# A decoder layer in fp32: opening reordered, fold spread over blocks, and the last two token blocks convolved as one block of 1024 tokens

## The chip, the cores and the metric

The kernel runs on one core of one Trainium2 chip. A core has five engines that run at the same time, each through its own fixed order of instructions: TensorE (PE) for matmuls, VectorE (DVE) and ScalarE (ACT) for elementwise work, GpSimd (POOL), and SyncE (SP), which here issues most transfers between the memory outside the core (DRAM) and the core's own SBUF. Matmul results land in PSUM, which has eight banks of 128 x 512 fp32. The metric is the device time of one execution in microseconds (us). A profile shows one execution of its own.

## The reference

`x` is 4096 tokens by 1024 columns, in fp32; `c` is one conditioning vector. What is computed:

```
mod = silu(c) @ w_ada + b_ada;  shift, scale, gate = split(mod, 3)
h    = layer_norm(x) * (1 + scale) + shift
proj = h @ w_in + b_in                    # u_a 512 | z_a 512 | glu 1024 | z_b 512
y_a  = (group_linear(causal_pool(u_a) - u_a) + b_pool) * ls_pool * silu(z_a)
v    = glu[:512] * sigmoid(glu[512:])
v    = silu(layer_norm(causal_depthwise_conv31(v)) * ln_conv_g + ln_conv_b)
y_b  = (v @ w_pw + b_pw) * silu(z_b)
y    = concat(y_a, y_b) @ w_out + b_out
out  = layer_norm(2**0.25 * x + gate * y) * ln_post_g + ln_post_b
```

The pool takes trailing windows of 2, 4, 8 and 16 tokens, one for each of four column groups; the convolution has 31 taps per column.

## The kernel before

**Numbers.** Matmuls keep fp32 accuracy by splitting each operand into a high half (a rounded cast, `hi`) and a low half (the rest, `lo`): each product is three matmuls, hi x hi, hi x lo and lo x hi (`mm3`). ACT casts the high half, DVE subtracts to get the low half (`split`, lines 194 to 196). Nearly all matmuls are 128 x 128 by 128 x 512.

**Stages.** The tokens are cut into 8 blocks of 512 (`sb`), each with its even and odd tokens apart. Columns lie on the 128 partitions.

1. *Opening.* The modulation `mod_block` multiplies the eight row tiles of `w_ada` by `silu(c)` on DVE (`macc`, line 181) and sums over the partitions with matmuls against ones (line 186). Block 0's x is transposed on PE and modulated (`mod_turned`, lines 321 to 324); its low half needs `hs` from ACT. Rows of `w_in` are loaded and split (`wg0` to `wg7`). PE runs the first matmuls of block 0 row by row as these arrive.
2. *First phase*, blocks 0 to 7: `row_stats` of the next block (mean and variance of each token by ACT, `col_stats`, then one transfer `rD` and a broadcast `xbc`), `norm_T` (a load `xk` of the transposed x, normalized by DVE at lines 292 and 294), `mod_xT` (high half on ACT, line 303, low half on DVE, line 304, giving the tile `x`), then 8 chunks of 24 matmuls for the glu (`p`), and 2 chunks for half of z_b (`p1z`). At the end of block 0, `fold_u` multiplies the pool weights into the first 512 columns of `w_in`: for each of four groups a load `wT`, eight small matmuls in fp32 `fv` (two passes each) and a bias `bu`. At block 1, `mod_gate` computes the gate on DVE.
3. *Second phase*, blocks 0 to 7: ten chunks of 24 matmuls (`p2z`, `p2u`, `p2b`); the pools run on DVE.
4. *Convolution* (`conv`), on DVE throughout the first two phases for the blocks in `BLOCKS`: three accumulation chains (even tokens, odd tokens, and sums of both; tiles `cx`, `ca`), some 46 multiply-adds (line 576) over 256 columns for one block or 512 for two. `conv_ln` transposes the result (`cl`), takes statistics on ACT, and applies the layer norm at lines 606 and 607. Blocks 6 and 7 are *late units*: eight pieces (block, column group) of 512 tokens, with tiles `lv` (input), `lx`, `la` (result). `EARLY = 2` of them stand ahead of the output stage, the others, by `PERSB`, one behind each of its blocks 0 to 5, and each block's layer norm behind its fourth unit.
5. *Output stage*, blocks 0 to 7: `pw_stage` (48 matmuls `pw`, z on DVE at line 696, halves `yb`), `prep` of the next block (loads `t`, halves `vp` and `ya`), and four `out_tile`s of 48 matmuls each into two PSUM banks (`po`). Four banks let two tiles be open. DVE adds the residual (lines 705 and 731) and applies the last layer norm (lines 744 and 745).

**What sets the order.** The program is written as one sequence; a scheduler orders each engine's instructions once, when the kernel is built, by its own estimate of times and the dependences. On the chip every engine runs its list in that order: an instruction that waits holds all that stand behind it. Tiles of one tag share slots, and the load of a new tile waits until the last reader of the slot's old tile is done. The late units' lines are these:

```
    late = {6: [], 7: []}
    units = [(sb, m) for sb in (6, 7) for m in range(MC)]
    for _ in range(EARLY):
        sb, m = units.pop(0)
        late_unit(sb, m, late[sb])
```

## Time and profile before

| | |
|---|---|
| Three runs | 1394.03, 1406.32, 1406.85 us (median 1406.32) |
| The profiled execution | 1397.84 us |
| Its span (first to last instruction) | 1395.8 us |
| Mean granted clock of PE, as a share of full | 0.992 |
| PE busy | 1356.4 us, 97% |
| DVE busy | 1193.9 us, 86% |
| ACT, POOL busy | 432.6 us, 131.0 us |
| DMA | 243.81 MB, mean 175 GB/s |

The page cuts the span into 40 slices of 35 us; each digit is the busy share in tenths, 9 meaning 90% or more:

```profile
PE   4898999999999999999999999999999999999997
...
DVE  8688989983569999899899699999997899998754
```

PE is busy nearly everywhere but in the first slices. Engine busy times are sums of instruction times; neighbouring instructions on PE and DVE overlap a little, so what one costs its engine is read from start to start. A wait is named by what was waited for: "PE p L337 <- ACT x L321" is a matmul of line 337 into tile p that waited for ACT's tile x of line 321.

### The profile page before, as it was taken

The page shows a single profiled execution, that of the slowest core. Times are in us where ns is not written, and L with a number is a line of the kernel's source. Part 1 is how long each engine was busy: PE and PEld are TensorE (multiplying, and loading weights), DVE is VectorE, ACT ScalarE, POOL GpSimd, SP SyncE. Part 2 cuts the span into 40 slices and gives each one's busy share as a digit, 9 for nine tenths or more (in the row PEclk, how much of TensorE's full clock was granted, in tenths as well). Part 3 has the DMA queues.
Part 4 walks back from the last instruction along what each step waited for, and adds up shares of the span by engine and source line. Part 5 has one row for each costly group of instructions (what it writes and reads, how often), then busy time and mean ns, then how long its engine had stood idle before and what let it go on. Part 6 is the DMA issues. An engine that isn't in the chain of part 4 may idle for free.

```text
span 1395.8 us, 17137 instructions
## 1 busy us (share of the span) xinstructions
PE 1356.4 (97%) x6045; PEld 1118.5 (80%) x6045; DVE 1193.9 (86%) x2348; ACT 432.6 (31%) x772; POOL 131.0 (9%) x193
## 2 busy tenths in 40 slices
PE   4898999999999999999999999999999999999997
PEld 3777888888888888888888888888888888888886
DVE  8688989983569999899899699999997899998754
ACT  3544235245531231411114111343234131322310
POOL 1000000010100001210111110100111101001111
PEclk9999999999999999999999999999999999999999
DMA  9958677477563662360541723466444443433511
GB/s 323 328 180 323 214 275 267 163 267 235 180 249 124 226 194 83 131 233 23 182 139 59 234 67 123 131 203 196 157 167 148 139 159 118 162 129 130 186 61 76
DMA packets 113352, 243.81 MB, mean 175 GB/s; under 512 B 15027, under 2 KB 45555, under 8 KB 113267
## 3 DMA queue, kind: packets, MB, share of 16 engines
q1 hardware_dynamic: 103984, 209.15, 43.4%
q0 software_dynamic: 9216, 33.56, 7.2%
q8 instruction: 47, 0.77, 0.2%
q14 instruction: 39, 0.31, 0.1%
q10 hardware_dynamic: 66, 0.02, 0.0%
HBM read 156.65 MB, written 86.04 MB: 174 GB/s over the span
## 4 chain that ended last, share of the span: by engine, by line
PE 90%; DMA 5%; DVE 2%; ACT 2%; SPq 1%; issue 1%; DVEq 0%; ACTq 0%
PE po L713 25%; PE p L338 6%; PE p L339 6%; PE p L337 6%; PE p2z L338 4%; PE p2u L338 4%; PE p2z L337 4%; PE p2z L339 4%; PE p2u L337 4%; PE p2u L339 4%; PE pw L689 2%; PE pw L691 2%; PE pw L690 2%; PE p2b L338 2%; PE p2b L337 2%; PE p2b L339 2%
## 5 line engine op out<-in xcount | busy, mean ns | idle before, releaser
L576 DVE SCALAR_TENSOR_TENSOR cx<-cv,wdw,cx 128x513 f32<-128x513 f32 (+1 forms) x240 | 145.7, 613 | 0.7
L576 DVE SCALAR_TENSOR_TENSOR ca<-cx,wsum,ca 128x256 f32<-128x256 f32 (+1 forms) x240 | 143.7, 611 | 0.1
L576 DVE SCALAR_TENSOR_TENSOR ca<-cv,wdw,ca 128x256 f32<-128x256 f32 (+1 forms) x224 | 134.3, 611 | 0.0
L742 POOL TENSOR_TENSOR ors<-ove,mhalf 128x1 f32<-128x1 f32 x32 | 46.9, 1467 | 408.8 <-DVE ove L738 400.4
L736 ACT ACTIVATE ojk<-r,osm 128x1024 bf16<-128x1024 f32 x31 | 35.6, 1148 | 148.3 <-DVE osm L733 148.3
L332 POOL DMA_DIRECT2D x2r<-xD x64 | 34.8, 544 | 402.8 <-PE p2b L339 276.7
L731 DVE SCALAR_TENSOR_TENSOR r<-po,r 128x512 f32<-128x512 f32 x62 | 40.9, 687 | 22.0 <-PE po L713 21.9
L576 DVE SCALAR_TENSOR_TENSOR lx<-lv,wdw,lx 128x257 f32<-128x257 f32 x120 | 57.5, 479 | 0.0
L576 DVE SCALAR_TENSOR_TENSOR la<-lx,wsum,la 128x256 f32<-128x256 f32 x120 | 57.3, 478 | 0.0
L576 DVE SCALAR_TENSOR_TENSOR la<-lv,wdw,la 128x256 f32<-128x256 f32 x112 | 53.3, 478 | 0.0
L269 POOL TENSOR_TENSOR xcs<-smx,mhalf 128x1 f32<-128x1 f32 x28 | 20.7, 740 | 343.9 <-DVE smx L268 343.6
L517 ACT ACTIVATE sz<-p2z,cols 128x512 f32<-128x512 f32 x32 | 22.0, 688 | 95.6 <-PE p2z L339 95.5
L292 DVE TENSOR_TENSOR xk<-xk,xbc 128x1024 f32<-128x1024 f32 x28 | 34.1, 1222 | 17.2 <-DMA xk<-in_x_t_dram 17.2
L303 ACT ACTIVATE x<-xk,shc 128x512 fp32r<-128x512 f32 x56 | 38.0, 719 | 31.5 <-DVE xk L294 31.5
L304 DVE SCALAR_TENSOR_TENSOR x<-xk,shc,x 128x512 fp32r<-128x512 f32 x56 | 40.4, 749 | 8.3 <-ACT x L303 8.3
L524 ACT ACTIVATE u<-p2u,bu 128x512 f32<-128x512 f32 x32 | 22.0, 689 | 70.4 <-PE p2u L339 70.4
L745 DVE SCALAR_TENSOR_TENSOR r<-r,ors,b_bc 128x1024 f32<-128x1024 f32 (+1 forms) x33 | 41.1, 1248 | 3.2 <-POOL ors L742 3.1
L443 ACT ACTIVATE sg<-p,cols 128x512 f32<-128x512 f32 x32 | 21.9, 686 | 70.3 <-PE p L339 69.8
L265 ACT ACTIVATE x<-x 128x1024 f32<-128x1024 f32 x28 | 29.6, 1059 | 40.6 <-DMA x<-in_x_dram 39.7
L713 PE MATMUL po<-wo0h,ya 128*128 128x512 f32 x128 | 41.2, 392 | 0.0
L713 PE MATMUL po<-wo1h,ya 128*128 128x512 f32 x128 | 41.1, 390 | 0.0
L705 DVE SCALAR_TENSOR_TENSOR r<-r,gbo 128x1024 f32<-128x1024 f32 x32 | 39.0, 1218 | 1.7 <-DMA r<-in_x_dram 1.7
(360 smaller groups left out, 4107.4 us busy)
## 6 DMA issues: line engine op xcount, KB each, us to landing
x2r<-xD POOLq DMA_DIRECT2D x64, 512.0 KB, 7.3
xD<-x SPq DMA_DIRECT2D x56, 512.0 KB, 5.4
x<-in_x_dram SPq DMA_DIRECT2D x32, 512.0 KB, 6.8
r<-in_x_dram SPq DMA_DIRECT2D x32, 512.0 KB, 3.6
out_dram<-r SPq DMA_DIRECT2D x31, 512.0 KB, 2.6
xk<-in_x_t_dram SPq DMA_DIRECT2D x28, 512.0 KB, 8.2
wa<-in_w_ada_dram SPq DMA_DIRECT2D x32, 256.0 KB, 6.4
vD<-v SPq DMA_DIRECT2D x32, 256.0 KB, 2.2
```

The lines of the kernel that those rows point to most:

```text
L303: nc.scalar.activation(h2[:, 0, :], z, AF.Identity, bias=shc[:, k : k + 1])
L304: nc.vector.scalar_tensor_tensor(h2[:, 1, :], z, shc[:, k : k + 1], h2[:, 0, :].bitcast(F32), op0=ALU.add, op1=ALU.subtract)
L337: nc.tensor.matmul(ps, w[0], X[0], start=first, stop=False)
L338: nc.tensor.matmul(ps, w[0], X[1], start=False, stop=False)
L339: nc.tensor.matmul(ps, w[1], X[0], start=False, stop=last)
L576: nc.vector.scalar_tensor_tensor(dst, src, wt, dst, op0=ALU.mult, op1=ALU.add)
L705: xg = nc.vector.scalar_tensor_tensor(r, r, ALPHA, gbo, op0=ALU.mult, op1=ALU.add)
L713: mm = nc.tensor.matmul(po[h], lhs, Wo[k][wi][:, h * 512 : (h + 1) * 512], start=(k == 0 and wi == 0 and lhs is yh), stop=last)
L731: nc.vector.scalar_tensor_tensor(r[:, sl], po[h], 1.0, r[:, sl], op0=ALU.mult, op1=ALU.add, accum_out=sm[:, h : h + 1])
L736: nc.scalar.activation(jk, r, AF.Square, bias=sm[:, 2:3], accum_out=ss)
L742: nc.gpsimd.tensor_tensor(rs, ve, mhalf[:, 0:1], op=ALU.pow)
L745: nc.vector.scalar_tensor_tensor(r[:, sl], r[:, sl], rs, b_bc[:, sl], op0=ALU.mult, op1=ALU.add)
```

## The change

The changed kernel differs in eight places. Line numbers of the changed file are some 3 to 20 higher.

1. **Modulation.** `mod_block` accumulates six of eight row tiles on DVE; the last two are added on PE as further matmuls into the same sum, so that there are three for each one before.
2. **Rows of w_in.** Each of the 8 loads takes three quarters of the columns and is cast and subtracted by one operation on each engine (before: two). The last quarter comes by 8 later transfers of 128 KB (`w3r`) and 16 splits.
3. **x of block 1** is loaded in the opening, into four slots of the tag `ca` (`x_early`).
4. **Statistics.** `col_stats` leaves out two DVE and one POOL operation per tile: the factors go into ACT's scale, and into `s1n` and `lcg`; one power per block on POOL (`inv_root`).
5. **Stores** of block 0's x to `xD` stand behind the `xk` loads of block 1, where they stood behind the last modulation.
6. **Fold.** The four `fold_u` stand one each in blocks 2 to 5 of the first phase, their loads `wT` one block earlier; they use another PSUM tag and another SBUF tag for `wf`.
7. **Gate.** `mod_gate` moves from block 1 of the first phase to block 2 of the second.
8. **Late convolution.** Four units, one for each column group, of 1024 tokens (blocks 6 and 7 together). Unit 0 stands right before the output loop, units 1 to 3 behind its blocks 0 to 2, then one layer norm for both blocks. `lv` and `lx` take two of the six `ca` slots, of which `vp` takes four. `EARLY` and `PERSB` are gone.

The core of the diff:

```diff
@@ mod_block
-        for kt in range(KT):
+        nv = KT - 2
+        for kt in range(nv):
...
-                nc.tensor.matmul(ps[:, nk * i + j : nk * i + j + 1], acc[:, 1 - i, j * P : (j + 1) * P],
-                                 ones[:, 0:1], start=True, stop=True)
+                o = ps[:, nk * i + j : nk * i + j + 1]
+                sl = slice(j * P, (j + 1) * P)
+                nc.tensor.matmul(o, acc[:, 1 - i, sl], ones[:, 0:1], start=True, stop=False)
+                for kt in range(nv, KT):
+                    nc.tensor.matmul(o, wts[kt][:, 1 - i, sl], sc[:, kt : kt + 1], start=False, stop=kt == KT - 1)
@@ col_stats
-        nc.scalar.activation(src, src, AF.Identity, accum_out=sm[:, 0:1])
-        nc.vector.tensor_scalar(nmean, sm[:, 0:1], -1.0 / n, None, op0=ALU.mult)
-        nc.scalar.activation(src, src, AF.Square, bias=nmean, accum_out=sm[:, 1:2])
-        nc.vector.tensor_scalar(sm[:, 2:3], sm[:, 1:2], 1.0 / n, EPS, op0=ALU.mult, op1=ALU.add)
-        nc.gpsimd.tensor_tensor(rstd, sm[:, 2:3], mhalf[:, 0:1], op=ALU.pow)
+        nc.scalar.activation(src, src, AF.Identity, scale=-1.0 / n, accum_out=nmean)
+        nc.scalar.activation(src, src, AF.Square, bias=nmean, scale=-float(n), accum_out=ss)
+
+    def inv_root(ss, n):
+        nc.gpsimd.tensor_scalar(ss, ss, n * EPS, None, op0=ALU.add)
+        nc.gpsimd.tensor_tensor(ss, ss, mhalf[:, : ss.shape[1]], op=ALU.pow)
@@ opening
+    x_early = []
+    for t in range(TT):
+        xt = s2.tile([P, D], F32, tag="ca", bufs=6, name=f"x{TT + t}", padded_shape=[P, 2 * (HQ + T + 1)])
+        nc.sync.dma_start(xt, tok(xv, TT + t))
+        x_early.append(xt)
...
+        hi, lo = (both(t)[:, :, : 3 * P] for t in Wg[k])
+        nc.scalar.copy(hi, rows[k])
         xT.append(mod_turned(pb, k))
-        split_cols(k, 0, 3)
-        split_cols(k, 3, 4)
+        nc.vector.tensor_tensor(lo, rows[k], hi.bitcast(F32), op=ALU.subtract)
...
+    for q in range(2):
+        raw = wraw(f"w3r{q}").rearrange("p (k h c) -> p k h c", k=4, h=2)
+        for k in range(4):
+            nc.sync.dma_start(raw[:, k], both(w_in[(4 * q + k) * P : (4 * q + k + 1) * P, 8 * P : 16 * P])[:, :, 3 * P :])
+        for k in range(4):
+            hi, lo = (both(t)[:, :, 3 * P :] for t in Wg[4 * q + k])
+            split(hi, lo, raw[:, k])
@@ first phase, end of a block
-            for g in range(MC):
-                fold_u(g, wpl)
-        if sb == 1:
-            mod_gate(gbo)
...
+        if 1 <= sb <= MC:
+            wT = wraw(f"wT{sb - 1}")
+            nc.sync.dma_start(wT, w_in_t[(sb - 1) * P : sb * P, :])
+        if 2 <= sb <= MC + 1:
+            fold_u(sb - 2, wpl, wTs.pop(0))
+        if 1 <= sb <= MC:
+            wTs.append(wT)
@@ late units
+    def late_unit(m):
+        a = (lt.tile([P, 2 * T], F32, tag="la", bufs=2, name=f"la{m}") if m < 2 else
+             s2.tile([P, 2 * T], F32, tag="cv", bufs=2, name=f"la{m}", padded_shape=[P, 2 * (HQ + T + 1)]))
+        v = s2.tile([P, 2, HQ + T + 1], F32, tag="ca", bufs=6, name=f"lv{m}")
+        tmp = s2.tile([P, 2 * T + HQ + 1], F32, tag="ca", bufs=6, name=f"lx{m}", padded_shape=[P, 2 * (HQ + T + 1)])
+        conv(m, 6, 2, v, tmp, a.rearrange("p (two i) -> p two i", two=2))
+        late.append(a)
...
+    late_unit(0)
     for sb in range(NSB):
...
-        for _ in range(PERSB[sb]):
-            if units:
-                q, m = units.pop(0)
-                late_unit(q, m, late[q])
-                if m == MC - 1:
-                    conv_ln(q, 1, late[q])
+        if sb < MC - 1:
+            late_unit(sb + 1)
+        if sb == MC - 2:
+            conv_ln(6, 2, late)
```

How instructions move is shown at three places. In these rows a name carries the serial number of its tile at its end; the rows are those of one engine, in its order.

**PE, between block 0 and block 1 of the first phase.** Before, the last rows of `p1z` are followed by the folds, with four matmuls of block 1 (`p_1`, which read `x_1_0`) between the first and the second:

```order
L339 MATMUL p1z_1_1016<-x_0_7_741,wz1l 128x512
L358 MATMUL fv_0_1069<-wpl,wT_1066 128x128 x4
L358 MATMUL fv_1_1075<-wpl,wT_1066 128x128 x4
L363 MATMUL bu_1082<-cols,wpl 128x1
L337 MATMUL p_1_8_1192<-x_1_0_962,wg0h 128x512
L337 MATMUL p_1_12_1193<-x_1_0_962,wg0h 128x512
L337 MATMUL p_1_9_1247<-x_1_0_962,wg0h 128x512
L337 MATMUL p_1_13_1248<-x_1_0_962,wg0h 128x512
L358 MATMUL fv_0_1088<-wpl,wT_1085 128x128 x4
L358 MATMUL fv_1_1094<-wpl,wT_1085 128x128 x4
```

Now block 1 follows at once:

```order
L346 MATMUL p1z_1_1038<-x_0_7_759,wz1l 128x512
L344 MATMUL p_1_8_1118<-x_1_0_968,wg0h 128x512
L344 MATMUL p_1_12_1119<-x_1_0_968,wg0h 128x512
L344 MATMUL p_1_9_1173<-x_1_0_968,wg0h 128x512
L344 MATMUL p_1_13_1174<-x_1_0_968,wg0h 128x512
```

The folds have left this place; the first of them now stands behind block 2's `p1z`.

**DVE, output stage, end of block 3.** The low half of `vp_3` belongs to the inputs of block 4's `pw` matmuls. Before, it stands between short operations of a late unit and ahead of the last two z of its own block (z_2 reads `pw_2` and `pw_3`):

```order
L576 SCALAR_TENSOR_TENSOR la_0_9271<-lx_0_9273,wsum,la_0_9271 128x256
L576 SCALAR_TENSOR_TENSOR lx_0_9273<-lv_0_9272,wdw,lx_0_9273 128x257
L696 SCALAR_TENSOR_TENSOR z_2_9377<-pw_2_9364,cols,z_2_9377 128x512
L576 SCALAR_TENSOR_TENSOR la_0_9271<-lv_0_9272,wdw,la_0_9271 128x256
L196 TENSOR_TENSOR vp_2_9415<-t_2_9412,vp_2_9415 128x512
L576 SCALAR_TENSOR_TENSOR la_0_9271<-lx_0_9273,wsum,la_0_9271 128x256
L196 TENSOR_TENSOR vp_3_9421<-t_3_9418,vp_3_9421 128x512
```

Now it stands at the end of the block, behind the reads of the block's fourth tile (`po_0_9461`, `po_1_9462`) and among the operations of the last two units, 512 columns each:

```order
L607 SCALAR_TENSOR_TENSOR la_9003<-lx_9005,wsum,la_9003 128x512
L617 SCALAR_TENSOR_TENSOR la_8565<-lx_8567,cols,la_8565 128x512
L607 SCALAR_TENSOR_TENSOR lx_9005<-lv_9004,wdw,lx_9005 128x513
L748 SCALAR_TENSOR_TENSOR r_9458,osm_9511<-po_0_9461,r_9458 128x512
L748 SCALAR_TENSOR_TENSOR r_9458,osm_9511<-po_1_9462,r_9458 128x512
L722 SCALAR_TENSOR_TENSOR r_9637<-r_9637,gbo 128x1024
L607 SCALAR_TENSOR_TENSOR la_9003<-lv_9004,wdw,la_9003 128x512
L762 SCALAR_TENSOR_TENSOR r_9391<-r_9391,ors_9453,b_bc 128x1024
L607 SCALAR_TENSOR_TENSOR la_9003<-lx_9005,wsum,la_9003 128x512
L607 SCALAR_TENSOR_TENSOR lx_9005<-lv_9004,wdw,lx_9005 128x513
L199 TENSOR_TENSOR vp_3_9238<-t_3_9235,vp_3_9238 128x512
```

The low half has moved from before the block's tiles to behind them.

**PE, output stage, where block 4's `pw` begins.** Before, the last tile of block 3 is followed by the rest of `pw_0` as one group, which reads `vp_3`:

```order
L713 MATMUL po_0_9644<-wo7h,yb_3_9397 128x512
L713 MATMUL po_1_9645<-wo7h,yb_3_9397 128x512
L689 MATMUL pw_0_9764<-vp_3_9421,wpw1h 128x512
L690 MATMUL pw_0_9764<-vp_3_9421,wpw1h 128x512
L691 MATMUL pw_0_9764<-vp_3_9421,wpw1l 128x512
L689 MATMUL pw_1_9783<-vp_0_9403,wpw0h 128x512
L690 MATMUL pw_1_9783<-vp_0_9403,wpw0h 128x512
```

Now `pw_0` and `pw_1` of block 4 are cut in pieces, and the ones that read `vp_3`'s low half (line 707) come behind the first halves of block 4's own first two tiles:

```order
L730 MATMUL po_1_9708<-wo3h,ya_3_9254 128x512
L707 MATMUL pw_0_9525<-vp_3_9238,wpw1h 128x512
L708 MATMUL pw_0_9525<-vp_3_9238,wpw1l 128x512
L707 MATMUL pw_1_9544<-vp_3_9238,wpw1h 128x512
L708 MATMUL pw_1_9544<-vp_3_9238,wpw1l 128x512
L706 MATMUL pw_2_9561<-vp_0_9220,wpw0h 128x512
L707 MATMUL pw_2_9561<-vp_0_9220,wpw0h 128x512
```

Both tiles' second halves, which read `yb`, stand behind these matmuls.

More of the change, by code (lines that the diff above doesn't have):

```diff
@@ L66, in tile_layer @@
     nc.vector.memset(ones, 1.0)
-    mhalf = cst.tile([P, 4], F32, name="mhalf")
+    mhalf = cst.tile([P, 2 * TT], F32, name="mhalf")
     nc.vector.memset(mhalf, -0.5)
@@ L247, in tile_layer @@
     s1 = cst.tile([P, KT], F32, name="s1")
+    s1n = cst.tile([P, KT], F32, name="s1n")
     shc = cst.tile([P, KT], F32, name="shc")
@@ L348, in inproj, with fold_u @@
         return banks
-    def fold_u(g, wpl):
-        wT = wraw(f"wT{g}")
-        nc.sync.dma_start(wT, w_in_t[g * P : (g + 1) * P, :])
-        wf = wraw(f"wf{g}")
+    wTs = []
+    def fold_u(g, wpl, wT):
+        wf = ph.tile([P, D], F32, tag="tm", bufs=5, name=f"wf{g}")
         for hb in range(2):
-            pb = s2_bank(f"fv{g}_{hb}")
+            pb = tp_bank(f"fv{g}_{hb}")
             for j in range(4):
@@ L391, in load_row, with both @@
         rows[k] = (wraw(f"wr{k}") if home < 2 else
-                   cst.tile([P, D], F32, tag=("gate", "gbo")[home - 2], name=f"wr{k}"))
-        nc.sync.dma_start(rows[k], w_in[k * P : (k + 1) * P, 8 * P : 16 * P])
+                   cst.tile([P, D], F32, tag=("gate", "gbo")[home - 2], name=f"wr{k}"))[:, : 6 * P].rearrange(
+                       "p (h c) -> p h c", h=2)
+        nc.sync.dma_start(rows[k], w_in[k * P : (k + 1) * P, 8 * P : 16 * P].rearrange(
+            "p (h c) -> p h c", h=2)[:, :, : 3 * P])
+    def both(t):
+        return t.rearrange("p (h c) -> p h c", h=2)
     mods = ((0, 1), (1, 1), (2, 2), (4, 2), (6, 2))
@@ L400, in tile_layer @@
             load_row(k)
-    def split_cols(k, m0, m1):
-        split(*(t.rearrange("p (h c) -> p h c", h=2)[:, :, m0 * P : m1 * P] for t in (*Wg[k], rows[k])))
+    x_early = []
[3 more added lines that the diff above has]
+        x_early.append(xt)
     xT = []
@@ L424, in tile_layer @@
     for q in range(2):
-        raw = wraw(f"wzr{q}")
+        raw = cst.tile([P, D], F32, tag=("gate", "gbo")[q], name=f"wzr{q}")
         nc.sync.dma_start(raw.rearrange("p (k n) -> p k n", k=4),
@@ L436, in tile_layer @@
     gbo = cst.tile([P, D], F32, tag="gbo", name="gbo")
-    for k in range(KT):
-        for i in range(2):
-            after(nc.sync.dma_start(xD[k][0][:, i, :], xT[k][i].bitcast(F32)), last, True)
     def glu(sb, m, pa, pg):
@@ L476, in tile_layer @@
         zs = norm_T(sb + 1, bc, 4) + norm_T(sb + 1, bc, 6)
+        if sb == 0:
+            for k in range(KT):
+                for i in range(2):
+                    after(nc.sync.dma_start(xD[k][0][:, i, :], xT[k][i].bitcast(F32)), x_loads[1])
         z_half(sb, xT)
         xT = xT_next + mod_xT(sb + 1, zs, 4)
-        if sb == 0:
+        if sb == 1:
             wpl = s2.tile([P, MC, P], F32, tag="cto", bufs=2, name="wpl")
@@ L554, in tile_layer @@
             nc.sync.dma_start(zD[1][sb][:, m - 2, :], sz)
+        if sb == GATE_SB:
+            mod_gate(gbo)
+            gb = wraw("gb")
+            nc.sync.dma_start(gb, b_ada[2 * D : 3 * D].partition_broadcast(P))
+            for h in range(2):
+                sl = slice(h * 512, (h + 1) * 512)
+                gp = tp_bank(f"gp{h}")
+                nc.tensor.matmul(gp, ones, gbo[:, sl], start=True, stop=True)
+                nc.vector.tensor_tensor(gate_bc[:, sl], gp, gb[:, sl], op=ALU.add)
+            nc.sync.dma_start(gbo, b_out.partition_broadcast(P))
+            nc.vector.tensor_tensor(gbo, gbo, gate_bc, op=ALU.mult)
     ph_ctx.close()
```

61 lines of the change are left out of this document (17 added, 44 removed).

## The prediction

> **What bounds the kernel now.** I read the profile in this order: the busy table of the page, a table of windows by stage, the waits of TensorE (PE), and last the timelines of the places that the change touches. The first shows the span and the busy time of each engine.
>
> ```profile
> span 1395.8 us, 17137 instructions
> ...
> PE 1356.4 (97%) x6045; PEld 1118.5 (80%) x6045; DVE 1193.9 (86%) x2348; ACT 432.6 (31%) x772; POOL 131.0 (9%) x193
> ```
>
> PE is idle for 1395.8 - 1356.4 = 39.4 us in all, so no edit can gain more than that plus what PE loses at a low clock. VectorE (DVE) is the second engine, 163 us below PE. The stages, with columns PE, PEld, DVE, ACT, POOL, granted clock, DMA share, GB/s:
>
> ```profile
> 93.50:137.60 44.10, 37.33 (x175) 32.03 (x174) 38.87 (x91) 22.71 (x40) 2.89 (x4) 0.85 0.79 276
> 137.60:400.00 262.40, 261.79 (x1161) 214.62 (x1160) 193.80 (x360) 108.64 (x180) 17.29 (x24) 1.00 0.65 228
> 400.00:950.00 550.00, 550.00 (x2467) 455.15 (x2466) 517.76 (x982) 141.02 (x279) 52.58 (x84) 1.00 0.45 149
> 950.00:1250.00 300.00, 300.00 (x1327) 247.10 (x1326) 278.95 (x574) 87.41 (x151) 32.19 (x24) 1.00 0.44 152
> ```
>
> From 137.6 to 1250 PE is hardly ever short of work, and a matmul takes 300 / 1327 = 0.226 us. All that can be gained lies before 137.6. But from 950 to 1250, the larger part of the output stage, DVE is busy for 279 of 300 us: there it hides behind PE by only 7%, and the last edit changes just this work. The two ends of the kernel are worth separate sums.
>
> **The opening and the fold.** The waits of PE (total us, times, longest):
>
> ```profile
> PE mod L186 <- DVE macc L181: 11.4, 2, 9.5
> PE fv L358 <- DMA wT<-in_w_in_t_dram: 4.8, 2, 4.5
> ...
> PE p L337 <- ACT x L321: 2.2, 2, 1.9
> PE p L338 <- DVE x L324: 2.2, 1, 2.2
> ```
>
> and the PE timeline where block 1 begins (start, us, instruction, wait before it), the last two rows being neighbours:
>
> ```profile
> 93.50 1.95 PE L358 MATMUL fv<-wpl,wT 128*128 128x128 f32 x16
> ...
> 108.42 3.76 PE L358 MATMUL fv<-wpl,wT 128*128 128x128 f32 x16 [4.49 <-DMA wT<-in_w_in_t_dram]
> ...
> 112.83 0.63 PE L338 MATMUL p<-x,wg0h 128*128 128x512 f32 x1
> 113.25 0.63 PE L339 MATMUL p<-x,wg0l 128*128 128x512 f32 x1
> ```
>
> Four folds of 16 small matmuls stand here in the queue, the third behind a load, and block 1's inputs come late. The first window shows what that costs: 44.1 - 37.3 = 6.8 us idle, and at a clock of 0.85 another 0.15 x 44.1 = 6.6 us, together 13 us. That is the upper bound of what spreading the fold can gain; the folds' own work, 4 x 1.95 = 8 us, comes again in blocks 2 to 5, where the second window has PE at 261.79 of 262.4. Whether the gain comes depends on x_1, block 1's normalized input. Its chain before the change, on SP's queue and on DVE:
>
> ```profile
> 82.62 2.06 SPq L291 DMA_DIRECT2D xk<-in_x_t_dram  x4
> ...
> 90.26 1.23 DVE L292 TENSOR_TENSOR xk<-xk,xbc 128x1024 f32<-128x1024 f32 x1
> ...
> 103.93 0.76 DVE L304 SCALAR_TENSOR_TENSOR x<-xk,shc,x 128x512 fp32r<-128x512 f32 x1
> ```
>
> The early loads of block 1's x and the stores of xD moved behind the xk loads let the statistics run in the opening. I put the xk issue 8 to 9 us earlier, at 73 to 75: its x tiles no longer wait behind the last weights, but the statistics still share ACT with the weights' casts. The first low half stood 103.93 - 82.62 = 21 us behind the issue, and keeps that: 96 to 98 (this is an estimate; the trace shows the old order alone). PE ends the z matmuls of block 0 at 93.5, or 1 to 2 earlier with the opening. So about 5 us of wait stay, and 13 - 5 = 8 us are gained. The PE waits for L321 and L324 (1.9 and 2.2) go with the whole-row split, but the late w3r rows now stand ahead of x_0_5 and x_0_6 on ACT and DVE, which I price at 1 to 2 us.
>
> The modulation's last two rows go to PE: 64 more matmul passes. Of these the trace has only rows for the present form:
>
> ```profile
> 56.88 0.95 PE L186 MATMUL mod<-ones,macc 128*128 128x1 f32 x8
> ```
>
> 0.95 / 8 = 0.12 us each, so 7.6 us, of which I take half to lie in the opening's idle time; DVE loses ten accumulations, two of them ahead of PE's first wait, worth 1 us there. The opening without the fold comes out even: 4 gained, 4 paid in matmuls, 1 to 2 for w3r, 1 for the earlier start. Together **-8 us**. Bounds: 13 + 4 = 17 gained if x_1 is in time; 3 if the xk loads are issued only where they are now and just the fold's own load wait of 4.5 goes, less the added matmuls.
>
> The gate's modulation moves into the second phase: PE is full in both places and DVE has 550 - 518 = 32 us free there, besides the two early convolution units that leave it. I take 0. The tile-wise statistics lose some 120 tiny DVE operations, spread over 400 us in which PE does not wait: 0.
>
> **The late convolution.** What one operation costs DVE is the step from one start to the next, since its operations overlap. Rows of the output stage, then a pair of 512-column operations in the second phase, then the low halves (two in one row), then the counts:
>
> ```profile
> 1160.02 1.28 DVE L745 SCALAR_TENSOR_TENSOR r<-r,ors,b_bc 128x1024 f32<-128x1024 f32 x1
> 1161.22 0.49 DVE L576 SCALAR_TENSOR_TENSOR lx<-lv,wdw,lx 128x257 f32<-128x257 f32 x1
> 1161.62 0.48 DVE L576 SCALAR_TENSOR_TENSOR la<-lv,wdw,la 128x256 f32<-128x256 f32 x1
> 1162.01 0.48 DVE L576 SCALAR_TENSOR_TENSOR la<-lx,wsum,la 128x256 f32<-128x256 f32 x1
> 1162.41 0.69 DVE L731 SCALAR_TENSOR_TENSOR r<-po,r 128x512 f32<-128x512 f32 x1
> ...
> 1163.63 1.22 DVE L705 SCALAR_TENSOR_TENSOR r<-r,gbo 128x1024 f32<-128x1024 f32 x1
> 1164.77 0.49 DVE L576 SCALAR_TENSOR_TENSOR lx<-lv,wdw,lx 128x257 f32<-128x257 f32 x1
> ```
>
> ```profile
> 508.12 0.76 DVE L576 SCALAR_TENSOR_TENSOR ca<-cv,wdw,ca 128x512 f32<-128x512 f32 x1
> 508.78 0.76 DVE L576 SCALAR_TENSOR_TENSOR ca<-cx,wsum,ca 128x512 f32<-128x512 f32 x1
> ```
>
> ```profile
> 1319.07 1.29 DVE L196 TENSOR_TENSOR vp<-t,vp 128x512 fp32r<-128x512 f32 x2
> 1320.28 1.22 DVE L705 SCALAR_TENSOR_TENSOR r<-r,gbo 128x1024 f32<-128x1024 f32 x1
> ```
>
> ```profile
> L576 DVE SCALAR_TENSOR_TENSOR lx<-lv,wdw,lx 128x257 f32<-128x257 f32 x120 | 57.5, 479 | 0.0
> L576 DVE SCALAR_TENSOR_TENSOR la<-lx,wsum,la 128x256 f32<-128x256 f32 x120 | 57.3, 478 | 0.0
> L576 DVE SCALAR_TENSOR_TENSOR la<-lv,wdw,la 128x256 f32<-128x256 f32 x112 | 53.3, 478 | 0.0
> ```
>
> Steps: 0.40 us at 256 columns, 0.66 at 512. A late unit has (120 + 120 + 112) / 8 = 44 of them: 44 x 0.40 = 17.5 us, with its few openers about 20. A unit of 1024 tokens has 44 x 0.66 = 29, with openers 33. Eight units were 158 us, four are 132: DVE is spared 26 us. But of the eight, two ran before the output stage and six were spread over its first six blocks; of the four, one starts ahead of the stage's first block and the others stand in blocks 0 to 2 of the loop, one each.
>
> A block of the output stage is 240 matmuls, 240 x 0.226 = 54.3 us of PE. DVE's other work in it: four tiles of 1163.63 - 1162.41 = 1.22 for the two halves of L731, 1.14 (L705), 1.20 (L745) and as much for its twin L744, together 4.8, so 19; twelve low halves at (1320.28 - 1319.07) / 2 = 0.60, so 7; four z at 0.66 and small ones, 3 to 4; in all 30. Before: 30 + 20 = 50 under 54.3. After: 30 + 33 = 63, which is 9 over, in each of the blocks that holds a unit. The first unit finds DVE's slack before the first tile. The other three put DVE 3 x 9 = 26 us back. What lies between the engines takes some of it: four PSUM banks, two tiles of 11 us. Walking both engines through their fixed orders by these steps, with each bank, low half and block's statistics waited for, the orders of before give no PE wait, as the trace has it. Those of after give PE waits of 17 us, 21 where each of the unit loads costs DVE 3 us, 35 where it costs 10. In the trace of before DVE waits for such loads twice, 3.0 us in all:
>
> ```profile
>   DMA lv<-vD: 3.0, 2
> ```
>
> The largest, 9 us together, stands in block 4: PE reaches pw_0 of that block, whose fourth input vp_3 has its low half behind operations of the last two units; the transposes of the third unit's result wait at the same place. Next come yb_0 of block 4 (3.6), and yb_2 and yb_3 of block 3 (3 to 5). ACT, which casts ahead of these low halves, is at 87 of 300 us and waits for PE rather than the reverse, so I cost it at 0. From block 5 on DVE is ahead again (its layer norm of the late block costs it 4 x (1.14 + 1.2) = 9 us and falls there). I take **+21**; the bounds are 4, where DVE never loses time to PE in blocks 0 to 2, and 35.
>
> A long wait also costs clock. After the 4.49 us wait the two neighbouring rows above are 113.25 - 112.83 = 0.42 us apart, not 0.226; the 6.6 us that the window lost to its clock fall on two such stretches, 3.3 us each. The 9 us wait is of this kind and part of its price is taken from the next wait: **+2**, bounds 0 and 7. [...]
>
> **Sum.** The profiled execution took 1397.84 us, 2.0 more than its span: 1397.84 - 8 + 21 + 2 = 1412.8. The three runs are 1394.03, 1406.32 and 1406.85, the profiled one 8.5 under their median and 4.6 under their mean. A run of the changed kernel may as well be of either kind, so I add 2, about half of the mean's distance: **1415**.
>
> **Rivals.**
> First, faster: DVE never makes PE wait, as its order lets units run while it waits for tiles. DVE's total falls by 26 us and more, and in the profile DVE does wait for PE's tiles between. It decides if the unit loads land unseen and DVE enters block 2 with all its lead, 9 us per block. Then only the opening counts, with up to 4 us left: 1397.84 - 8 + 2 = 1392. Against it: 63 over 54.3 holds whatever the order.
>
> Second, slower: the loads of the late units. Each unit's first operation stands in DVE's queue with the tiles' reads behind it, and its slot comes free only when DVE or PE is done with the previous owner, so the load can't start early. At 10 us each (twice the bytes of before, with other transfers in flight) the walk gives 35: 1397.84 - 8 + 35 + 5 + 2 = 1432. It decides above some 5 us each. Against it: only 3.0 us in two waits now.
>
> Third: the fold's spreading does not bring x_1 earlier, as the loads of 128 KB and of x fill the queue in the opening. Then the opening is worth 3: 1397.84 - 3 + 21 + 2 + 2 = 1420.
>
> **How the numbers follow.** Forecast 0.5, its own range 1402 to 1425; no PE wait 0.24; the loads 0.15; no gain in the opening 0.11. A measurement of this kernel tells about 1%, 14 us, from no change, and the forecast lies 21 + 2 - 8 = 15 us over before on like terms, just at that edge. So of the forecast's 0.5 I count 0.26 within 1%, as the runs' own spread is as wide, and 0.24 slower; of the first rival 0.17 within and 0.07 faster, where x_1 is in time (17 gained); the second rival slower; of the third 0.04 within, 0.07 slower. Faster 0.07, within 0.47, slower 0.46. The range 1391 to 1432 reaches from the first rival to the second.
>
> **What would show it.** In the changed profile: no fold at 93 to 137, the clock in that window above 0.85, and x_1's first low half before 100; PE waits for vp, yb and the transposes in the fourth and fifth block of the output stage, between 1110 and 1240, 15 to 25 us together, DVE full in the windows from 1000 to 1200 and under 70% from 1250; a low clock after the longest wait. PE without waits from 950 on would prove the largest term wrong; lv waits of over 15 us on DVE would name the second rival; an xk issue still after 80 the third.

## The result and the profile after

The changed kernel took 1409.88 us (median of 17 runs, 1408.54 to 1412.43) beside 1405.25 of the kernel before in the same session (1393.62 to 1408.69): a ratio of 1.0059, 95% interval 1.0037 to 1.0081. It is 0.6% slower, which lies within the 1% that the prediction took as "no change". Here and beside the last three experiments the runs of the kernel before fall into two groups, 1394 to 1400 us (as the profiled one) and 1404 to 1409, beside the others nearly all are near 1396: between experiments compare times and spans, not ratios. The profiled execution took 1409.23 us, its span is 1407.4; the profiled one of before took 1397.84, with a span of 1395.8. All sums below compare these two spans, 11.6 us apart.

First the page of the changed kernel: the span, the busy times, and PE's and DVE's slices of 35 us.

```profile
span 1407.4 us, 16815 instructions
...
PE 1368.1 (97%) x6108; PEld 1127.5 (80%) x6108; DVE 1151.7 (82%) x2004; ACT 433.0 (31%) x771; POOL 113.7 (8%) x157
...
PE   5989998999999999999999999999999989999997
...
DVE  7589998752419999989999789789999999957654
```

DVE has 42 us less work than before and the kernel is slower all the same. The stages again, with the columns of the prediction's table (PE, PEld, DVE, ACT, POOL, granted clock, DMA share, GB/s), then three 50 us pieces of the output stage:

```profile
93.50:137.60 44.10, 40.28 (x171) 32.54 (x170) 41.44 (x90) 18.72 (x30) 1.58 (x2) 0.96 0.77 281
137.60:400.00 262.40, 256.49 (x1169) 212.13 (x1168) 176.05 (x303) 107.71 (x177) 16.78 (x10) 0.99 0.58 210
400.00:950.00 550.00, 550.00 (x2463) 454.27 (x2462) 490.61 (x844) 145.24 (x292) 41.33 (x72) 1.00 0.48 162
950.00:1250.00 300.00, 294.22 (x1287) 240.47 (x1286) 290.84 (x480) 83.95 (x148) 30.41 (x20) 0.99 0.40 140
...
1100.00:1150.00 50.00, 47.58 (x209) 38.43 (x207) 50.00 (x80) 11.01 (x19) 5.80 (x4) 1.00 0.42 143
1150.00:1200.00 50.00, 46.88 (x193) 37.74 (x194) 50.00 (x84) 11.09 (x18) 5.81 (x4) 0.93 0.25 89
1200.00:1250.00 50.00, 49.76 (x228) 40.71 (x227) 43.28 (x74) 21.17 (x45) 5.79 (x4) 1.00 0.47 167
```

Two windows carry the news. In the first, PE's idle time fell from 6.8 to 3.8 us and the clock rose from 0.85 to 0.96: the opening did gain. But the second, in which PE was full before, now holds 5.9 us of idle time. In the output stage DVE is busy for all of 1100 to 1200, and PE is not.

PE's waits (total us, times, longest) name the places:

```profile
PE ccp L72 <- POOL ccs L273: 4.5, 1, 4.5
PE po L730 <- DVE r L748: 3.6, 1, 3.6
...
PE p L344 <- ACT sgz L477: 3.1, 1, 3.1
PE pw L706 <- DVE z L713: 2.7, 2, 1.6
...
PE xcp L72 <- POOL xcs L273: 1.4, 1, 1.4
PE p L345 <- DVE x L311: 0.7, 1, 0.7
```

To see where time goes in a kernel whose bound engine is full nearly everywhere, count its large matmuls. There are 5760 of 128 x 512 in both kernels, in the same stages. The start of the n-th, changed minus before, measured from the span's start, is:

| n-th large matmul | place | difference, us |
|---|---|---|
| 1st | first of block 0 | +1.2 |
| 241st | block 1 begins | -3.6 |
| 601st | in block 2 | -16.4 |
| 841st | block 3 | -6.2 |
| 1681st | block 7 begins | -1.4 |
| 3841st | output stage begins | +0.5 |
| 4681st | fourth output block | -1.0 |
| 4801st | fourth to fifth output block | +6.2 |
| 5161st | sixth output block | +12.0 |
| last | | +11.7 |

So 16.4 us are gained by block 2 and all of them are gone before the output stage; the stage then loses 11.2 us.

**The first loss.** The timeline of POOL, then that of PE, of the changed kernel around 240 (start, us, instruction, wait):

```profile
232.61 4.52 POOL L272 TENSOR_SCALAR xcs<-xcs 128x4 f32<-128x4 f32 x1 [60.20 <-ACT x L269]
237.22 1.04 POOL L273 TENSOR_TENSOR xcs<-xcs,mhalf 128x4 f32<-128x4 f32 x1
238.23 6.19 POOL L272 TENSOR_SCALAR ccs<-ccs 128x4 f32<-128x4 f32 x1
244.51 1.04 POOL L273 TENSOR_TENSOR ccs<-ccs,mhalf 128x4 f32<-128x4 f32 x1
```

```profile
238.31 0.27 PE L72 MATMUL xcp<-ident,xcs 128*8 128x128 f32 x1 [1.43 <-POOL xcs L273]
245.60 0.27 PE L72 MATMUL ccp<-ident,ccs 128*8 128x128 f32 x1 [4.48 <-POOL ccs L273]
```

These are the two operations of `inv_root`. An add over 128 x 4 took 4.52 and 6.19 us, and PE, which turns the result into rows, stood behind both: 1.43 + 4.48 = 5.9 us, the idle time of the second window. Where POOL was free of whatever held it, the same add took 0.23 us (a row of that size is shown below). After the wait the clock was low:

```profile
245.80:249.20 3.40, 3.40 (x10) 2.62 (x9) 3.21 (x4) 0.00 (x0) 0.00 (x0) 0.50 0.99 385
1150.30:1157.10 6.80, 5.56 (x13) 4.40 (x14) 6.80 (x16) 0.75 (x2) 0.00 (x0) 0.50 0.03 11
99.00:102.40 3.40, 3.17 (x8) 2.50 (x9) 3.40 (x8) 1.39 (x2) 0.00 (x0) 0.50 1.01 398
```

Half the clock for 3.4 us is 1.7 us of work; together 7.6 us. The sum up to the output stage closes within 1 us: -16.4, + 7.4 for the four folds that now stand in blocks 2 to 5 (from the steps between the large matmuls around them), + 7.6, + 1.3 for the gate's matmuls, is -0.1, and + 0.5 was measured. Folds and gate are no loss: the kernel before had done both by the 601st matmul. What the opening gained is 16.4 - 7.4 - 1.3 = 7.7 us, and the two waits for POOL with their clock took 7.6 of it away.

**The second loss.** PE's timeline in the output stage, the two longest waits:

```profile
1151.54 0.79 PE L730 MATMUL po<-wo0h,ya 128*128 128x512 f32 x1 [3.63 <-DVE r L748]
...
1191.96 0.50 PE L706 MATMUL pw<-vp,wpw0h 128*128 128x512 f32 x1 [1.58 <-DVE z L713]
```

The first is the last tile of the fourth block, waiting for the PSUM bank that DVE has not read yet; the stretch at half clock (the middle row above) lasts 6.8 us, of which 1.2 lie in the wait itself, so it is worth 5.6 / 2 = 2.8 us. Waits of 6.8 us in all (3.6 and 2.7 in the list above, and 0.3 and 0.2 for low halves) and 2.8 of clock are 9.6 of the 11.2. (Some 3 us of the step from the 4801st to the 5161st matmul are transposes of the late blocks, which the kernel before has at other places; at the last matmul they cancel.) Why is DVE that late? Its first operation into the result tile of late unit 0, and PE's first matmul of the output stage:

```profile
943.22 0.48 DVE L605 TENSOR_SCALAR la<-lv,wdw 128x512 f32<-128x512 f32 x1
```

```profile
946.95 0.39 PE L706 MATMUL pw<-vp,wpw0h 128*128 128x512 f32 x1
```

Unit 0, some 33 us of DVE's time, was meant to run ahead of the stage. It begins 3.7 us ahead of it. I call this distance the head start.

### The profile page after: what moved, and what is told of

It is laid out like the page before. It is cut to its first block, busy times and chain, and to the rows that moved or that the text cites. A ratio compares the mean times of both kernels' runs of the same rounds, so it can differ in the third digit from the quotient of the medians.

```text
span 1407.4 us, 16815 instructions
## 1 busy us (share of the span) xinstructions
PE 1368.1 (97%) x6108; PEld 1127.5 (80%) x6108; DVE 1151.7 (82%) x2004; ACT 433.0 (31%) x771; POOL 113.7 (8%) x157
## 4 chain that ended last, share of the span: by engine, by line
PE 81%; DVE 10%; DMA 4%; issue 1%; ACT 1%; POOL 1%; SPq 1%; DVEq 0%; ACTq 0%; POOLq 0%
PE po L730 15%; PE p L345 8%; PE p L344 7%; PE p L346 7%; PE p2z L344 4%; PE p2u L344 4%; PE p2u L345 4%; PE p2z L346 4%; PE p2u L346 4%; PE p2z L345 4%; DVE la L607 2%; PE p2b L344 2%; PE p2b L346 2%; PE p2b L345 2%; PE p1z L345 2%; PE p1z L344 2%
## 5 line engine op out<-in xcount | busy, mean ns | idle before, releaser
L607 DVE SCALAR_TENSOR_TENSOR cx<-cv,wdw,cx 128x257 f32<-128x257 f32 (+1 forms) x240 | 145.2, 612 | 1.2
L464 DVE SCALAR_TENSOR_TENSOR v<-p,cols,sg 128x512 f32<-128x512 f32 x32 | 23.7, 745 | 71.2 <-ACT sg L462 66.7
L687 ACT ACTIVATE t<-t,cols 128x512 f32<-128x512 f32 x32 | 22.8, 724 | 84.3 <-DMA t<-tD 78.7
L198 ACT CAST yb<-z 128x512 fp32r<-128x512 f32 x32 | 19.8, 619 | 81.9 <-DVE z L713 62.3
L607 DVE SCALAR_TENSOR_TENSOR lx<-lv,wdw,lx 128x513 f32<-128x513 f32 x60 | 44.8, 747 | 0.0
L607 DVE SCALAR_TENSOR_TENSOR la<-lx,wsum,la 128x512 f32<-128x512 f32 x60 | 44.7, 746 | 0.0
L730 PE MATMUL po<-wo2h,ya 128*128 128x512 f32 x128 | 42.7, 393 | 0.0
```

The lines of the kernel that those rows point to most:

```text
L607: nc.vector.scalar_tensor_tensor(dst, src, wt, dst, op0=ALU.mult, op1=ALU.add)
L730: mm = nc.tensor.matmul(po[h], lhs, Wo[k][wi][:, h * 512 : (h + 1) * 512], start=(k == 0 and wi == 0 and lhs is yh), stop=last)
```

## The experiments

The theories for the stage's loss: (T1) four units of 1024 tokens overload blocks 0 to 2, whatever else is done, so part 8 alone costs it; (T2, formed after the first four runs) DVE comes too late to unit 0, because parts 6 and 7 delay the background convolution, and the head start decides. For the loss near 240: (S1) `inv_root`'s form on POOL is slow; (S2) POOL is held up by what DVE does at the time. Ratios are to the kernel before in the same session, with 95% intervals; the changed kernel was not run again beside the experiments. "Stage" is the time from the first pw matmul to the last po matmul; it is 441.1 us before and 452.3 in the changed kernel.

**Part 8 alone.** The kernel before, with only its late units replaced:

```diff
-EARLY = 2
-PERSB = (1, 1, 1, 1, 1, 1, 0, 0)
...
+    late_unit(0)
     for sb in range(NSB):
...
+        if sb < MC - 1:
+            late_unit(sb + 1)
+        if sb == MC - 2:
+            conv_ln(6, 2, late)
```

> The kernel before with part 8 alone (late convolution as four units of 1024 tokens). Theory, DVE overload: the loss of the output stage comes from part 8 alone. The output stage gets waits of PE for DVE and a low clock of 10 to 13 us together, while the start of the output stage stays at 947 us: profiled time about 1398 + 11 = 1409, waits on r, z, yb or vp 6 to 9 us from 950 on. Rival, other parts: if the statistics or the gate cause the loss, PE has no waits from 950 on and the time is that of the kernel before.

Measured: 1397.43 us, ratio 1.0001 (0.9987 to 1.0015). The stage took 442.2 us, 1.1 more than before; PE waits for DVE 0.6 us in all. Unit 0 had a head start of 35.7 us. T1 falls, and the expectation's rival came true: the same four units in the same three blocks cost nothing here.

**All but part 8.** The changed kernel with the eight late units of before:

```diff
+EARLY = 2
+PERSB = (1, 1, 1, 1, 1, 1, 0, 0)
...
-    late_unit(0)
     for sb in range(NSB):
```

> The changed kernel with the eight late units of before (parts 1 to 7 alone). Theory: no PE wait from 950 on, the output stage begins at 947 as in both, time about 1409.9 - 11 = 1399 for this kernel; the POOL operation of several us and the PE wait for it near 240 stay. Rival: the output stage loses its 10 us without part 8 too, and the time stays near 1410.

Measured: 1420.3 us, ratio 1.0172 (1.0155 to 1.0189): the expectation missed, by some 20 us. The wait near 240 is there as in the changed kernel, and the output stage opens with a new one. From its list of PE's waits, the new one and the POOL one:

```profile
PE po L747 <- ACT ya L200: 9.1, 1, 9.1
PE ccp L74 <- POOL ccs L275: 5.9, 2, 4.5
```

Unit 0 starts early here (869), but ahead of the last background block's layer norm, which comes at 958 in place of 926. The load of `ya` stands behind that layer norm's transfers in SP's queue, and goes out at 960.55 (928.29 in the changed kernel). So part 8 is not what makes the change slow. With the other seven it is even the better of the two.

**The add of `inv_root` on DVE** in place of POOL, in the changed kernel:

```diff
-        nc.gpsimd.tensor_scalar(ss, ss, n * EPS, None, op0=ALU.add)
+        nc.vector.tensor_scalar(ss, ss, n * EPS, None, op0=ALU.add)
```

> The changed kernel with the small addition of the grouped statistics (128 x 4 or 128 x 8) on DVE in place of POOL; POOL keeps the power. [...] Rival, ACT's chain of statistics is what is late: the PE waits for ccp and xcp stay at 4 us or more under another name.

Measured: 1408.44 us, ratio 1.0086 (1.0071 to 1.0102). PE's waits near 240 are gone, and the output stage starts 6.4 us earlier than before (the two waits and their clock had cost 7.6). But the stage takes 459.0 us, 17.8 more than before, with a head start of 0.7 us. PE's waits there:

```profile
PE po L730 <- DVE r L748: 7.2, 2, 3.7
```

This is the plainest sight of T2: what PE gains early only brings it sooner to a point for which DVE is late.

**The add on ACT**, as an activation with a bias:

```diff
+        nc.scalar.activation(ss, ss, AF.Identity, bias=(epsx if n == D else epsc)[:, 0:1])
```

> The changed kernel with the same addition on ACT, so that POOL's power is released by ACT, at any point of DVE's stream. [...] Rival, only the tensor_scalar form is slow on POOL: every power takes 1 to 2 us, and the PE waits for POOL go, 6 to 9 us gained.

Measured: 1404.79 us, ratio 1.0063 (1.0048 to 1.0078); stage 454.5 us, head start 4.7. Now the power itself, which alone of the two is left on POOL, took 6.12 us at 174.65 and 2.40 at 241.9, where 1.04 is its usual time, and PE waited 2.6 us for the first. So it is not the add's form: S1 falls. In the changed kernel DVE ran convolution operations without a gap beside both slow adds. Rows of DVE's timeline there, with the two that break the run, v (which reads PSUM) and xk (which waited for a load):

```profile
236.29 0.75 DVE L607 SCALAR_TENSOR_TENSOR ca<-cv,wdw,ca 128x512 f32<-128x512 f32 x1
236.96 0.75 DVE L464 SCALAR_TENSOR_TENSOR v<-p,cols,sg 128x512 f32<-128x512 f32 x1
237.62 0.75 DVE L607 SCALAR_TENSOR_TENSOR ca<-cx,wsum,ca 128x512 f32<-128x512 f32 x1
...
243.58 0.75 DVE L607 SCALAR_TENSOR_TENSOR ca<-cx,wsum,ca 128x512 f32<-128x512 f32 x1
245.99 1.22 DVE L299 TENSOR_TENSOR xk<-xk,xbc 128x1024 f32<-128x1024 f32 x1 [1.66 <-DMA xk<-in_x_t_dram]
```

The first slow add ended at 232.61 + 4.52 = 237.13, in the v row; the second at 238.23 + 6.19 = 244.42, as DVE's run ended. The other traces agree: in the eight with the add on POOL, all twelve adds over 128 x 4 that took more than 2 us ended 0.1 to 0.2 us after DVE had begun a v or ended its run. But two earlier adds of the changed kernel, which also fell into a run of convolution operations without a gap, were quick:

```profile
121.13 0.46 POOL L272 TENSOR_SCALAR xcs<-xcs 128x4 f32<-128x4 f32 x1 [62.25 <-ACT x L269]
...
170.84 0.37 POOL L272 TENSOR_SCALAR xcs<-xcs 128x4 f32<-128x4 f32 x1 [48.04 <-ACT x L269]
```

So S2 fits the way in which the slow operations end; why some in such a run are not held stays open. It was not tried by itself, with a gap put into DVE's run alone, and no run shows how DVE would hold POOL: the slow adds (4.52 and 6.19 us) agree with it, the quick ones (0.46 and 0.37 us) do not.

**The fold's tile `wf` in another tag**, since in `tm` it takes a slot that the loads of x need:

```diff
-        wf = ph.tile([P, D], F32, tag="tm", bufs=5, name=f"wf{g}")
+        wf = wraw(f"wf{g}")
```

> The changed kernel with one thing back: the fold's result tile wf in the tag wraw, as before, and not among the five slots of tm that the x tiles and xk use. Theory, the convolution's late start: with wf out of tm, the x loads of block 7 stand ahead of the xD stores again, the layer norm of the first convolved block starts near 400 us and not at 420, the convolution's second block ends its second group near 445 and not 464, the first late unit starts near 915 and not 943, and PE's waits for DVE after 950 shrink from 6.9 us to under 3: 1410 - 8 = about 1402. Rival, the gate: DVE is late because of the gate's 9 us in the second phase; then the layer norm may come earlier but the first late unit still starts after 930 and the time stays at 1408 or more.

Measured: 1399.55 us, ratio 1.0026 (1.0016 to 1.0037), 10.3 us less than the changed kernel. The chain that this shortens is seen in the changed kernel's SP, ACT and DVE timelines:

```profile
390.39 2.29 SPq L264 DMA_DIRECT2D x<-in_x_dram  x3
392.78 0.38 SPq L368 DMA_DIRECT2D uD<-wf  x1
```

```profile
411.59 0.25 ACT L279 COPY rowsc<-ccp 8x128 f32<-8x128 f32 x1
```

```profile
420.39 2.50 DVE L638 TENSOR_TENSOR ca<-ca,cbc 128x512 f32<-128x512 f32 x4 [0.21 <-DMA cbc<-cD]
```

Before, the loads of x for the last block were issued at 356 to 365, and ACT's copy and the first convolution block's layer norm stood here:

```profile
393.46 0.25 ACT L275 COPY rowsc<-ccp 8x128 f32<-8x128 f32 x1
```

```profile
400.08 2.50 DVE L606 TENSOR_TENSOR ca<-ca,cbc 128x512 f32<-128x512 f32 x4 [8.56 <-DMA cbc<-cD]
```

In the changed kernel these loads of x wait for slots of `tm` until 390; ACT takes the x statistics ahead of the copy, and the layer norm comes 20 us late. The next convolution operations start at 433.5 (413.4 before), and the convolution stays behind by 17 us to its end (895 against 878). With `wf` elsewhere the layer norm is back at 399 and the end at 870, the head start is 25.9 us and the stage 448.9, as the theory had it. But the span is 9.4 us shorter than the changed kernel's, and only 3.4 of it lie in the stage. The other 6.1 lie ahead of it, where the two adds on POOL now come at 221.64 and 233.56 and take 2.50 and 0.23 us, and PE's waits for them are gone (0.5 us for a later one is left, at 276). So this run takes away both losses at once.

**Both of these**, `wf` in the other tag and the add on DVE:

```diff
-        nc.gpsimd.tensor_scalar(ss, ss, n * EPS, None, op0=ALU.add)
+        nc.vector.tensor_scalar(ss, ss, n * EPS, None, op0=ALU.add)
...
-        wf = ph.tile([P, D], F32, tag="tm", bufs=5, name=f"wf{g}")
+        wf = wraw(f"wf{g}")
```

> The changed kernel with wf in the tag wraw and the small addition of the statistics on DVE. Theory: the two gains add, as the convolution is no longer late when PE arrives sooner: POOL's wait near 240 is gone, the output stage begins near 939, PE waits under 4 us for DVE there, 1391 to 1397. Rival, DVE's own work in the output stage sets the end wherever it starts: PE arrives sooner and waits longer, 1403 or more.

Measured: 1398.4 us, ratio 1.001 (0.9994 to 1.0026), a miss by 1.4 us: the gains do not add, since with `wf` alone PE no longer waited for POOL near 240. Head start 25.8 us, stage 449.1: the same as with `wf` alone. That the head start, and not the POOL wait, goes with the stage's loss is seen from the run with the add on DVE alone, where the wait is gone and the stage is worse.

**The fold back at the end of block 0**, all four, as before, in the changed kernel:

```diff
+        if sb == 0:
...
+            for g in range(MC):
+                fold_u(g, wpl)
...
-        if 2 <= sb <= MC + 1:
-            fold_u(sb - 2, wpl, wTs.pop(0))
```

> The changed kernel with the whole fold at the end of block 0 again, as before. Theory: the opening loses its gain of 8 us at 93 to 137, so PE is 14 to 16 us less ahead at 140 us than in the changed kernel but does no fold later (8 us); the layer norm of the first convolved block starts near 400, the first late unit near 915, and the output stage loses under 4 us; together about 1403 to 1408, with the POOL wait near 240 kept. Rival, the spread is what pays: time 1415 or more.

Measured: 1390.76 us, ratio 0.9969 (0.9956 to 0.9982), 19 us less than the changed kernel: the fold's spreading, with its tags, is what makes the change slow. The expectation missed by 12 us and its rival by more: it had the opening's gain go with the fold, and the gain stays. The window at block 1's beginning:

```profile
93.50:137.60 44.10, 44.10 (x226) 37.35 (x225) 43.56 (x103) 19.93 (x36) 5.17 (x2) 1.00 0.87 318
```

PE has no idle time there and the full clock, with folds at 93.0, 108.9, 125.9 and 136.8 by the timeline. Block 1's input is in time: its first low half starts at 92.73 (98.43 in the changed kernel), its xk loads at 75.0 (78.2). At the 481st matmul this kernel is 13.6 us ahead of before with all folds done, the changed one 15.3 with none. The layer norm of the first convolution block comes at 385, the head start is 25.2 us and the stage takes 447.4. POOL's add was slow here too, out of PE's way, and quick one block later:

```profile
118.77 4.12 POOL L272 TENSOR_SCALAR xcs<-xcs 128x4 f32<-128x4 f32 x1 [59.64 <-ACT x L269]
...
170.56 0.23 POOL L272 TENSOR_SCALAR xcs<-xcs 128x4 f32<-128x4 f32 x1 [46.54 <-ACT x L269]
```

**The gate back** in block 1 of the first phase, in the changed kernel:

```diff
+        if sb == 1:
+            mod_gate(gbo)
...
-        if sb == GATE_SB:
-            mod_gate(gbo)
```

> The changed kernel with the gate in block 1 of the first phase again, as before. Theory, the convolution is late by the layer norm of its first block: that stays near 420, the first late unit starts after 930, and the output stage loses 8 us or more again: 1407 to 1412. Rival, the gate's DVE work in the second phase makes the convolution late: the first late unit starts before 925 and the time falls to 1402 or less.

Measured: 1397.34 us, ratio 1.0015 (1.0003 to 1.0026): the theory missed and the rival came true. The first layer norm is still late (415), yet the second stands at 607 in place of 629, unit 0 has 21.0 us of head start and the stage takes 449.6. Between these two layer norms the changed kernel has the gate's multiply-adds on DVE (514 to 546). So the gate's DVE work in the second phase is part of the delay.

**Unit 0 alone moved**, in the changed kernel: it stands right behind the last background layer norm in the program, ahead of the preparation of output block 0.

```diff
         late.append(a)

+    late_unit(0)
...
     b_bc = ph.tile([P, D], F32, name="b_bc", bufs=1)
     nc.sync.dma_start(b_bc, ln_post_b.partition_broadcast(P))
-    late_unit(0)
```

> The changed kernel with only one thing moved: late unit 0 stands right behind the last background convolution's layer norm in the program, ahead of the preparation of output block 0, instead of right ahead of the output loop. Theory (the head start of unit 0 before PE's first pw matmul decides the loss): unit 0 starts at about 905 to 920 in place of 943, the head start grows from 4 to 27 to 40 us, and PE loses 1 to 8 us in the output stage in place of 11; time 3 to 10 us below the changed kernel's, about 1398 to 1406. Rival A (the loss belongs to units 1 to 3 and their slots, whatever unit 0 does): loss still 10 to 12, time 1407 to 1411. Rival B (unit 0 now stands ahead of the low halves of w_pw, w_out and vp on DVE, which makes the output stage start later): stage begins 5 us or more later, time 1410 or more.

Measured: 1411.49 us, ratio 1.0065 (1.0038 to 1.0092): rival B. Unit 0 now starts at 878, the last background layer norm at 945 (926 in the changed kernel), and the load of `ya` behind it at 949.43. PE's first wait of the stage:

```profile
PE po L731 <- ACT ya L198: 5.6, 1, 5.6
```

By the count of matmuls this kernel lies 15.5 us behind the kernel before at the 121st matmul of the stage, and 15.4 at the last: from there on it loses nothing on balance. The same late convolution that cost the changed kernel 11.2 us is free once unit 0 is out of the way, but here DVE had no room ahead of the stage, so the loss moved to the stage's door.

**Fold back and unit 0 moved:**

```diff
+            for g in range(MC):
+                fold_u(g, wpl)
...
         late.append(a)

+    late_unit(0)
```

> The changed kernel with the fold back at the end of block 0 (the kernel that took 1390.8) and with late unit 0 moved ahead of the preparation of output block 0. Theory (head start decides): the fold at block 0 leaves PE 14 us ahead at the output stage's start; unit 0 starts at 870 to 885 in place of 908, where DVE stood idle for 16 us, the head start is 45 us or more, and the stage loses 0 to 3 us in place of 6.3; time 1384 to 1388. Rival A (the loss belongs to units 1 to 3): 1390 to 1392. Rival B (the output stage starts later since the halves stand behind unit 0): 1393 or more.

Measured: 1383.88 us, ratio 0.9853 (0.9823 to 0.9884), the fastest of all, and T2's number within 0.2 us. Its span is 14.7 us shorter than that of before. The page's span and busy times, all of PE's waits that the list has, unit 0's first row and the first `pw`:

```profile
span 1381.1 us, 16797 instructions
...
PE 1358.3 (98%) x6108; PEld 1122.8 (81%) x6108; DVE 1150.4 (83%) x2004; ACT 432.0 (31%) x771; POOL 112.3 (8%) x157
```

```profile
PE mod L188 <- DVE macc L181: 9.7, 2, 8.6
PE vpsa L72 <- DMA vrowsa<-in_b_in_dram: 3.0, 1, 3.0
PE cps L72 <- POOL corr L133: 2.3, 1, 2.3
```

```profile
842.64 0.49 DVE L600 TENSOR_SCALAR la<-lv,wdw 128x512 f32<-128x512 f32 x1 [0.39 <-DMA lv<-vD]
```

```profile
932.09 0.40 PE L702 MATMUL pw<-vp,wpw0h 128*128 128x512 f32 x1
```

No wait is left beyond the opening. The stage takes 440.8 us, and DVE's busy time is that of the changed kernel (1150.4 and 1151.7).

**Fold and gate both back:**

```diff
+            for g in range(MC):
+                fold_u(g, wpl)
+        if sb == 1:
+            mod_gate(gbo)
```

> The changed kernel with both the fold and the gate back where the kernel before had them (fold at the end of block 0, gate at the end of block 1 of the first phase). Theory (DVE's progress decides, and the gate's 8 multiply-adds of 128 x 1024 and three small ones, some 11 us of DVE, are then done early): DVE stands the same in sum, unit 0 starts within 905 to 915 as without this step, the stage loses 4 to 8 us, time 1389 to 1394. Rival (the gate in the second phase is what costs, as the comparison of the changed kernel with the one with the gate back alone suggests: 12 us): unit 0 starts at 895 or before, loss 0 to 4, time 1380 to 1387.

Measured: 1394.45 us, ratio 0.9934 (0.9908 to 0.9961), 3.7 us more than with the fold back alone, though its ratio is smaller. Unit 0 starts at 900, the head start is 42.2 us and the stage takes 441.2: no loss. Before that, though, PE waits 4.0 and 1.7 us for block inputs (`p` for DVE's and ACT's x), and the stage begins only 4.2 us ahead of before in place of 13.7. So the gate in the first phase costs PE 9.5 us ahead of the stage here, and its absence from the second phase gives 6.2 back in it; neither theory of the expectation had that.

All in one table, from the first row of `la` on DVE and the first of `pw` on PE in each trace, one profiled execution each:

| kernel | head start, us | stage minus before's 441.1, us |
|---|---|---|
| add on DVE | 0.7 | 17.8 |
| changed | 3.7 | 11.2 |
| add on ACT | 4.7 | 13.4 |
| gate back | 21.0 | 8.5 |
| fold back | 25.2 | 6.3 |
| `wf` and add moved | 25.8 | 8.0 |
| `wf` moved | 25.9 | 7.8 |
| part 8 alone | 35.7 | 1.1 |
| fold and gate back | 42.2 | 0.1 |
| fold back, unit 0 moved | 89.4 | -0.3 |

The two kernels whose stage opens late, with PE waiting for `ya` behind the last layer norm (all but part 8, unit 0 alone moved), are left out. At 36 us and more, about a unit's own 33, the loss is gone or 1 us. Below that the head start orders the kernels only roughly: 3.7 us go with less loss than 4.7, and near 25 us the loss is 6.3 to 8.0.

## Why the prediction was right in the time, and wrong in its parts

The time: 1415 against a median of 1409.88, inside the range, and "within 1%" was the likeliest of its three. On like terms the sum was 1412.8 for the profiled execution, which took 1409.23. But two of its terms were wrong by about 9 and 12 us, in opposite directions; that their sum came so near is luck. The + 2 for the runs' spread did not come either: the changed kernel's median lies 0.7 us over its profiled execution.

**Opening and fold, -8: measured + 0.5.** What the prediction said of block 1's beginning held. With the folds' 8 us taken out it amounts to 16 gained there, and 16.4 were (1.3 of them the gate, which was still to come). The xk loads were issued at 78.2, not 73 to 75, and the first low half stood 20.2 us behind them at 98.43 (predicted 21, and 96 to 98). PE's wait for the modulation fell by 2 us, from 11.4 to 9.4. What failed is the sentence on the tile-wise statistics, "spread over 400 us in which PE does not wait: 0". It counted the operations taken away and not the chain that takes their place: one add and one power per block on POOL, at the end of the block's statistics, with PE's transpose behind them. That chain was priced at nothing and cost 7.6 us. The gate, also "0", cost PE nothing, since its 1.3 us of matmuls only moved; but on DVE it cost more than it seemed: 17 us of head start, by the run with the gate back.

**Late convolution, + 21, and clock, + 2: measured 11.2 together.** DVE is indeed the bound from about 1100 to 1200 (busy for 50.00 of 50.00 us in both windows), and the longest waits went with half the clock (3.4 us of it behind the one of 4.5, 6.8 at the one of 3.6). The size was half of what was forecast, and the place another. The 9 us at vp_3 did not come; the longest was 3.6 us for the bank of `r` in the fourth block, then 1.6 at z. The clock's 2.8 us lay within its bounds. Two steps failed. One is "The first unit finds DVE's slack before the first tile". It did not: the background convolution ended 17 us late and unit 0 had a head start of 3.7 us. The other is "The other three put DVE 3 x 9 = 26 us back". In the kernels where the first sentence is true, with a head start of 36 us or more, the three units cost 1.1, 0.1 and -0.3 us, and not 17 to 35. They do not fill three blocks: with part 8 alone their rows run from 988 to 1207. These 219 us are four blocks of 54.3 us, for which the prediction's own figures give 4 x 30 + 3 x 33 = 219 us of DVE (an estimate), so nothing is over. With the first sentence true the term is near 0, as these kernels show; the 11 us came from a delay that it did not foresee, and that they were half of the forecast is chance. They belonged not to part 8 by itself but to part 8 behind parts 6 and 7, which the term never named.

**The rivals.** The first (DVE never makes PE wait) is what part 8 does by itself. Its condition, "enters block 2 with all its lead", was the right one, and parts 6 and 7 took the lead away. The second, unit loads of 10 us, did not occur: the list of DVE's waits in the changed kernel has none for `lv`. The third came nearest to the opening's worth at the stage's door, but by another cause than a late x.

## What to carry to other kernels

An engine that is busy for 82% of the span can still be the bound in one stage. What decides there is how far ahead it enters the stage, so ask of each moved piece whether it delays that engine's background work, even hundreds of us earlier. A tile put into a shared tag delays the loads that wait for its slots; here one slot of `tm` at 390 us turned into a late convolution at 895. And work that becomes "fewer operations" must be priced by the chain that is left, not by the count that goes: batching 4 small results into one puts that one on the path.
